# Low parts of split weights: an accumulating DMA onto a negated high part, in place of a subtraction on GpSimd

## The chip, the cores and the metric

The kernel runs on one core of a Trainium2 chip. The metric is the device time of one execution in microseconds, as a median of runs. The core has five engines that run side by side, each through its own queue in order: TensorE (PE, matrix products into PSUM, an accumulator memory), VectorE (DVE), ScalarE (ACT), GpSimd (POOL) and SyncE (SP, which here only issues DMAs). SBUF is the working memory on the core. The DMAs of all queues run on the same 16 DMA engines.

## The reference

One inference step of a transformer-like layer on 128 context tokens and 1024 latent tokens with 1024 channels. Cut to what matters here:

```
h    = rmsnorm(x, w_norm1) * (1 + scale1) + shift1
proj = h @ w_in                       # q, k, v, u (conv branch), g (gates)
o    = differential attention(q, k, v), 4 heads, then rmsnorm
cv   = silu(layernorm(dwconv31(glu(u))))
merged = sigmoid(g_a) * (o @ w_attn_proj) + sigmoid(g_b) * (cv @ w_conv_proj)
x    = x + gate1 * (merged @ w_out)
h    = rmsnorm(x, w_norm2) * (1 + scale2) + shift2
up   = dwconv3(h @ w_up)
x    = x + gate2 * ((silu(up_a) * up_b) @ w_down)
y    = rmsnorm(x, w_final)
```

All inputs and outputs are float32.

## The kernel before

Every product with weights is done in three passes of a fast format, fp32r: each operand is split into a high part (`hi`, the value rounded to fp32r) and a low part (`lo`, the rest), and `mm3` adds hi x hi, lo x hi and hi x lo in PSUM. The 1152 tokens stand in three chunks of 384 columns, n = 0, 1, 2.

Weights come as units of 128 x 1024 floats (512 KB), in the fixed order `SEQ` of 126 units: q0, k0 (first projections), ua0, ub0, ua1, ub1 (conv branch), v0 to v3, then 22 units that fill PE between the steps of attention, 4 more gate units, m0 to m7 (merge), wo0 to wo7 for the chunks 0 and 1, wo0 to wo7 a second time for chunk 2, and 66 units of the FFN (fa, fb: the two halves of w_up; d: w_down). A unit is normally 8 blocks x 3 chunks x 3 passes = 72 matmuls of 384 columns. In the first pass over wo it is 48, in the second pass 24. Counted from 0, v3 is unit 9, the second pass is units 52 to 59, and fa0, fb0, fa1, fb1 are units 60 to 63.

How a unit gets ready: `fetch_to` has SP load it into one of two `raw` buffers. `prep_to` (L153 to L155) has ACT copy raw into one of three `whi` buffers, which rounds it, and has POOL subtract, `lo = raw - hi`, into one of three `wlo` buffers (DVE does this for the first two units). The last unit's two parts stand in another buffer and are named `wlast`. A raw buffer is free for the next load when the lo part is done. A whi or wlo buffer is free when PE is done with the unit that is three earlier. `take` hands a unit to PE, and after the first chunk's matmuls (in the first pass over wo after chunk 0, in the second pass after the only chunk) `prep_to` is called for the unit two further on.

What else stands around it: in the attention stage DVE and POOL share a depthwise convolution of 31 taps (L611 on DVE, L618 on ACT with L624 on POOL). From the merge on, `ada2` (L1159) computes the remaining modulation vectors on DVE from 32 loads named `araw` that ACT's queue issues (L1148), with a custom multiply-and-sum of two operands. `resid` (L1186) adds a PSUM result to x on DVE, `square` sums squares on ACT (L1196) and DVE (L1197). `h2` makes the normalised FFN input, chunk by chunk. In the FFN `up_evac` (L1284) copies PSUM into `up` on ACT, and `glue` runs the width-3 convolution on DVE.

The order in which each engine's instructions stand is set when the program is built: a scheduler takes the code's order, its own model of how long each operation takes, and the priorities of `hp` in attention; `pin` then holds some engines close to the code's order.

Of the kernel before, what the change touches and what calls it, by code (L numbers as in the profile page):

```python
# [8 lines left out]
F32 = mybir.dt.float32  # L9
F32R = mybir.dt.float32r  # L10
AF = mybir.ActivationFunctionType
ALU = mybir.AluOpType
# [100 lines left out]
class Kernel:  # L113
# [28 lines left out]
    def prep_to(self, p):  # L142
        nc = self.nc
        while self.prepped < min(p, len(SEQ)):
            self.fetch_to(self.prepped + 1)
            raw = self.raw.pop(0)
            if self.prepped < len(SEQ) - 1:
                hi = self.wp.tile([128, 1024], F32R, tag="whi", name="whi", bufs=3)
                lo = self.wp.tile([128, 1024], F32R, tag="wlo", name="wlo", bufs=3)
            else:  # L150
                both = self.hb.tile([128, 3, 1024], F32R, tag="hb", name="wlast")
                hi, lo = both[:, 0], both[:, 1]
            nc.scalar.copy(hi, raw)  # L153
            eng = nc.vector if self.prepped < 2 else nc.gpsimd
            eng.tensor_tensor(out=lo, in0=raw, in1=hi.bitcast(F32), op=ALU.subtract)  # L155
            self.w[self.prepped] = (SEQ[self.prepped], hi, lo)
            self.prepped += 1
        self.fetch_to(self.prepped + self.fetch_ahead)
# [1402 lines left out]
```

## Time and profile before

| | us |
|---|---|
| three timed runs | 1835.44, 1835.63, 1837.52 (median 1835.63) |
| the profiled execution's own time | 1837.85 |
| its span, first to last instruction | 1836.0 |
| PE busy in it | 1726.6 (94%) |
| DVE busy | 1211.2 (66%) |
| POOL busy | 714.3 (39%) |
| ACT busy | 606.4 (33%) |

Busy time of an engine is the union of its instructions' time. Matmuls are pipelined: each row is longer than the distance to the next one, so busy PE says that something was under way. Waits and the issue of DMAs are not counted as busy. PE's granted clock has two levels, 1.2 and 2.4 GHz; a figure of 1.00 is the higher one throughout, 0.5 the lower.

### The profile page before, as it was taken

What the parts mean: (1) busy time and instruction counts of PE and PEld (TensorE: products, weight loads), DVE (VectorE), ACT (ScalarE), POOL (GpSimd) and SP (SyncE); (2) the same over time, 40 slices, a digit from 0 to 9 for tenths busy, and PEclk for the clock granted to TensorE, in tenths of its full rate; (3) what the DMA queues carried; (4) which work ended last, traced back from release to release, by engine and by line L of the source; (5) the groups of instructions that cost most, each with busy time, mean ns of one, the idle gap of its engine ahead of it and who ended that gap; (6) DMA issues with size and microseconds to landing.
All of it is one profiled execution on the core that took longest, in us unless ns stands there. A gap on an engine that the chain in (4) does not pass through costs nothing. (4 is left out here: it accounts for less than half of the span.)

```text
span 1836.0 us, 25204 instructions
## 1 busy us (share of the span) xinstructions
PE 1726.6 (94%) x10138; PEld 1685.5 (92%) x10138; DVE 1211.2 (66%) x1515; ACT 606.4 (33%) x1097; POOL 714.3 (39%) x466
## 2 busy tenths in 40 slices
PE   5989889989989999899978999999999999999997
PEld 3889889979889999799977999999999999999997
DVE  5858985697795762765989855464454635545366
ACT  4424454354553563212233312222122221221222
POOL 2545772674772422543243322222222322223231
PEclk8999999999999999999989999999999999999999
DMA  8264233433325325555641211111111111111102
GB/s 314 76 185 154 83 92 104 139 87 104 118 79 195 115 94 202 195 188 195 236 146 59 79 46 46 35 46 46 35 47 46 36 46 42 40 46 40 41 24 104
DMA packets 86172, 184.05 MB, mean 100 GB/s; under 512 B 8196, under 2 KB 56232, under 8 KB 84008
## 3 DMA queue, kind: packets, MB, share of 16 engines
q1 hardware_dynamic: 33888, 101.27, 17.0%
q10 hardware_dynamic: 51592, 79.08, 13.5%
q8 instruction: 80, 1.31, 0.3%
q0 software_dynamic: 576, 2.10, 0.3%
q14 instruction: 36, 0.29, 0.1%
HBM read 142.80 MB, written 39.60 MB: 99 GB/s over the span
## 5 line engine op out<-in xcount | busy, mean ns | idle before, releaser
L155 POOL TENSOR_TENSOR wlo<-raw,whi 128x1024 fp32r<-128x1024 f32 x123 | 309.9, 2521 | 631.8 <-ACT whi L153 524.0
L203 PE MATMUL f<-h1h,whi 128*128 128x384 f32 x680 | 232.6, 344 | 4.1 <-ACT gt L574 3.4
L203 PE MATMUL f<-h1l,whi 128*128 128x384 f32 x680 | 233.6, 344 | 0.0
L203 PE MATMUL f<-h1h,wlo 128*128 128x384 f32 x680 | 231.4, 341 | 0.0
L153 ACT CAST whi<-raw 128x1024 fp32r<-128x1024 f32 x125 | 131.3, 1051 | 299.5 <-PE f L203 123.6
L611 DVE SCALAR_TENSOR_TENSOR conv<-glu,vec,conv 128x967 f32<-128x967 f32 x120 | 199.4, 1661 | 1.1
L1289 DVE TENSOR_SCALAR ya<-up,vec 128x1153 f32<-128x1153 f32 x22 | 54.3, 2466 | 180.8 <-ACT up L1284 177.0
L203 PE MATMUL f<-h2h,whi 128*128 128x384 f32 x416 | 141.4, 340 | 6.0 <-ACT up L1284 3.7
L203 PE MATMUL T<-h2h,whi 128*128 128x384 f32 x432 | 144.4, 335 | 0.0
L203 PE MATMUL T<-h2l,whi 128*128 128x384 f32 x432 | 144.3, 334 | 0.0
L203 PE MATMUL T<-h2h,wlo 128*128 128x384 f32 x432 | 144.1, 334 | 0.0
L624 POOL TENSOR_TENSOR conv<-conv,tap 128x200 f32<-128x200 f32 x120 | 115.3, 961 | 68.6 <-ACT tap L618 66.1
L203 PE MATMUL f<-h2l,whi 128*128 128x384 f32 x416 | 140.9, 339 | 0.1
L203 PE MATMUL f<-h2h,wlo 128*128 128x384 f32 x416 | 140.5, 338 | 0.0
L203 PEld LDWEIGHTS f<-h1h,whi 128*128 128x128 f32 x680 | 129.7, 191 | 5.7 <-ACT gt L574 4.0
L203 PEld LDWEIGHTS f<-h1l,whi 128*128 128x128 f32 x680 | 130.0, 191 | 0.4
L203 PEld LDWEIGHTS f<-h1h,wlo 128*128 128x128 f32 x680 | 129.6, 191 | 0.2
L1305 POOL TENSOR_TENSOR fl<-ya,fh 128x128 fp32r<-128x128 f32 (+1 forms) x44 | 63.0, 1431 | 156.7 <-ACT fh L1304 156.7
L753 DVE TENSOR_REDUCE mx<-S 128x1 f32<-128x1152 f32 (+1 forms) x72 | 88.6, 1231 | 31.1 <-PE S L747 31.1
L1186 DVE SCALAR_TENSOR_TENSOR x<-f,g,x 128x384 f32<-128x384 f32 (+2 forms) x154 | 75.0, 507 | 48.6 <-PE f L203 45.3
L755 ACT ACTIVATE e<-S,mx 128x1152 f32<-128x1152 f32 (+1 forms) x72 | 81.3, 1129 | 70.1 <-DVE mx L753 52.7
L1289 DVE TENSOR_SCALAR yb<-up,vec 128x1153 f32<-128x1153 f32 x22 | 56.2, 2554 | 69.3 <-ACT up L1284 69.3
(332 smaller groups left out, 4651.0 us busy)
## 6 DMA issues: line engine op xcount, KB each, us to landing
raw<-in_wst SPq DMA_DIRECT2D x126, 512.0 KB, 3.6
araw<-in_ada ACTq DMA_DIRECT2D x32, 512.0 KB, 3.7
scr_gscr<-gate ACTq DMA_DIRECT2D x48, 192.0 KB, 2.0
tg<-scr_gscr SPq DMA_DIRECT2D x24, 384.0 KB, 3.9
ada<-in_ada SPq DMA_DIRECT2D x8, 1024.0 KB, 9.9
K<-scr_kscr ACTq DMA_DIRECT2D x4, 1920.0 KB, 8.8
V<-scr_vscr ACTq DMA_DIRECT2D x4, 1280.0 KB, 7.2
scr_vscr<-e ACTq DMA_DIRECT2D x36, 128.0 KB, 1.9
```

The lines of the kernel that those rows point to most:

```text
L153: nc.scalar.copy(hi, raw)
L155: eng.tensor_tensor(out=lo, in0=raw, in1=hi.bitcast(F32), op=ALU.subtract)
L203: nc.tensor.matmul(out, lhsT=a, rhs=b, start=(i == 0), stop=(i == n - 1))
L611: t = nc.vector.scalar_tensor_tensor(out=o, in0=glu[:, j:j + CSPLIT], scalar=w[:, j:j + 1], in1=o, op0=ALU.mult, op1=ALU.add)
L624: t = nc.gpsimd.tensor_tensor(out=o, in0=o, in1=p, op=ALU.add)
L753: nc.vector.tensor_reduce(out=mx[:, 1:2], in_=src, axis=AX.XY, op=ALU.min)
L755: nc.scalar.activation(out=e[:, :w].rearrange("p (a b) -> p a b", a=nk), in_=src, func=AF.Exp, scale=-1.0, bias=mx[:, 1:2], accum_out=self ...
L1186: nc.vector.scalar_tensor_tensor(out=d, in0=ps[:, o:o + ln], scalar=gate[:, j, c:c + 1], in1=d, op0=ALU.mult, op1=ALU.add)
L1289: nc.vector.tensor_scalar(out=y[:, :L], in0=u[:, 0:L], scalar1=w[:, 0:1], scalar2=None, op0=ALU.mult)
L1305: nc.gpsimd.tensor_tensor(out=fl[:, d:d + ln], in0=ya[:, s:s + ln], in1=fh[:, d:d + ln].bitcast(F32), op=ALU.subtract)
```

## The change

From the third unit on, the lo part is no longer computed by POOL. ACT writes minus the hi part into the lo buffer, and POOL's queue issues a DMA from raw to lo that adds to what stands there: lo = -hi + raw.

```
-            eng = nc.vector if self.prepped < 2 else nc.gpsimd
-            eng.tensor_tensor(out=lo, in0=raw, in1=hi.bitcast(F32), op=ALU.subtract)
+            if self.prepped < 2:
+                nc.vector.tensor_tensor(out=lo, in0=raw, in1=hi.bitcast(F32), op=ALU.subtract)
+            else:
+
+                nc.scalar.activation(out=lo, in_=hi.bitcast(F32), func=AF.Copy, scale=-1.0)
+                nc.gpsimd.dma_start(out=lo.bitcast(F32), in_=raw, accum_op=ALU.add)
```

Lines behind L155 have numbers that are higher by 4 in the changed kernel (L155 becomes L158 for the negation and L159 for the DMA).

The scheduler moves instructions with it. Below are three places.

ACT in the first units of the second pass over wo. The first CAST is the hi copy of unit 52, the others those of 53 and, in the first list, 54; `sq` are the squares of L1196, `araw` the loads of L1148. Before:

```order
L153 CAST whi_8408<-raw_8264 128x1024
L1148 DMA araw_8325<-in_ada2 128x1024
L1196 ACTIVATE sq_8366<-x1_1_7911 128x384
L1148 DMA araw_8327<-in_ada2 128x1024
L1196 ACTIVATE sq_8405<-x1_0_7910 128x384
L1148 DMA araw_8399<-in_ada2 128x1024
L153 CAST whi_8478<-raw_8338 128x1024
L1196 ACTIVATE sq_8440<-x1_1_7911 128x384
L1148 DMA araw_8401<-in_ada2 128x1024
L1196 ACTIVATE sq_8475<-x1_0_7910 128x384
L1148 DMA araw_8908<-in_ada2 128x1024
L153 CAST whi_8558<-raw_8412 128x1024
```

In the changed kernel, from the hi copy of unit 52 (whi_8458) to that of 54 (whi_8610); L158 is the negation:

```order
L153 CAST whi_8458<-raw_8313 128x1024
L1152 DMA araw_8374<-in_ada2 128x1024
L158 ACTIVATE wlo_8459<-whi_8458 128x1024
L1200 ACTIVATE sq_8416<-x1_1_7955 128x384
L1152 DMA araw_8376<-in_ada2 128x1024
L1200 ACTIVATE sq_8455<-x1_0_7954 128x384
L153 CAST whi_8529<-raw_8388 128x1024
L1152 DMA araw_8449<-in_ada2 128x1024
L158 ACTIVATE wlo_8530<-whi_8529 128x1024
L1200 ACTIVATE sq_8491<-x1_1_7955 128x384
L1152 DMA araw_8451<-in_ada2 128x1024
L153 CAST whi_8610<-raw_8463 128x1024
```

For units 52 and 53 the issue of an araw load stands between the hi copy and the negation.

ACT at the begin of the FFN. The first CAST is the hi copy of unit 63, fb1; `up` are copies out of PSUM. Before:

```order
L1148 DMA araw_9129<-in_ada2 128x1024
L153 CAST whi_9191<-raw_8904 128x1024
L1284 COPY up0_8912<-f_9084 128x384
L153 CAST whi_9195<-raw_9144 128x1024
L1284 COPY up1_8913<-T_9112 128x384
```

In the changed kernel:

```order
L1152 DMA araw_9189<-in_ada2 128x1024
L153 CAST whi_9252<-raw_8964 128x1024
L1288 COPY up0_8972<-f_9144 128x384
L153 CAST whi_9257<-raw_9205 128x1024
L1288 COPY up1_8973<-T_9172 128x384
L158 ACTIVATE wlo_9253<-whi_9252 128x1024
L158 ACTIVATE wlo_9258<-whi_9257 128x1024
```

The negation of fb1 stands behind two copies out of PSUM and the hi copy of the next unit.

POOL near unit 9, v3. The CAST of v3 is on ACT; here stand the tap additions of the convolution and the subtraction (before) or the issue of the DMA. Before:

```order
L624 TENSOR_TENSOR conv_926<-conv_926,tap_1301 128x200
L624 TENSOR_TENSOR conv_926<-conv_926,tap_1319 128x200
L155 TENSOR_TENSOR wlo_1398<-raw_966,whi_1397 128x1024
L624 TENSOR_TENSOR conv_926<-conv_926,tap_1335 128x200
L155 TENSOR_TENSOR wlo_1556<-raw_1167,whi_1555 128x1024
```

In the changed kernel:

```order
L628 TENSOR_TENSOR conv_931<-conv_931,tap_1342 128x200
L628 TENSOR_TENSOR conv_931<-conv_931,tap_1358 128x200
L159 DMA wlo_1405<-raw_972 128x1024
L628 TENSOR_TENSOR conv_931<-conv_931,tap_1377 128x200
L628 TENSOR_TENSOR conv_931<-conv_931,tap_1398 128x200
L159 DMA wlo_1564<-raw_1174 128x1024
```

The issue for v3 stands one tap addition later than the subtraction did.

## Rows read from the trace of the kernel before

**Rows 1.** The page's head and its first part: busy us of each engine, share of the span, and number of instructions.

```profile
span 1836.0 us, 25204 instructions
PE 1726.6 (94%) x10138; PEld 1685.5 (92%) x10138; DVE 1211.2 (66%) x1515; ACT 606.4 (33%) x1097; POOL 714.3 (39%) x466
```

**Rows 2.** Busy time by stage: begin and end in us, length, then busy us (and instructions) of PE, PE's weight loads, DVE, ACT and POOL, PE's granted clock, the DMA engines' busy share, GB/s. The stages are the first projections, attention, merge, the passes over wo with the begin of the FFN, and the rest of the FFN.

```profile
0.00:190.00 190.00, 158.88 (x1004) 145.33 (x1005) 137.18 (x178) 74.86 (x139) 85.48 (x83) 0.95 0.53 179
190.00:735.00 545.00, 510.62 (x3130) 495.20 (x3129) 398.12 (x456) 264.18 (x514) 291.05 (x199) 0.99 0.38 118
735.00:880.00 145.00, 131.95 (x734) 127.87 (x733) 98.15 (x133) 33.10 (x48) 65.38 (x45) 0.99 0.61 203
880.00:1040.00 160.00, 139.78 (x744) 135.64 (x743) 145.72 (x206) 53.48 (x89) 60.33 (x30) 0.91 0.41 126
1040.00:1836.00 796.00, 785.41 (x4534) 781.50 (x4532) 432.03 (x545) 180.79 (x308) 212.03 (x111) 0.99 0.14 45
```

**Rows 3.** The page's costliest groups, those of the two lines that make hi and lo: line, engine, operation, tiles, shape, count; busy us and mean ns of one; idle time of the engine just before them and what ended most of it.

```profile
L155 POOL TENSOR_TENSOR wlo<-raw,whi 128x1024 fp32r<-128x1024 f32 x123 | 309.9, 2521 | 631.8 <-ACT whi L153 524.0
L153 ACT CAST whi<-raw 128x1024 fp32r<-128x1024 f32 x125 | 131.3, 1051 | 299.5 <-PE f L203 123.6
```

**Rows 4.** PE's waits over the whole span: us in total, times, longest.

```profile
PE S L225 <- DVE mod L1159: 6.0, 1, 6.0
...
PE f L203 <- POOL wlo L155: 1.4, 1, 1.4
```

**Rows 5.** DMAs of 512 KB each. Two rows of line L1137, POOL's own plain DMAs (issue on POOL, min/median/max ns), and the time from issue to landing of the four; then, from the page's list of DMA issues, the raw loads on SP's queue with the median us to landing.

```profile
L1137 POOL DMA_DIRECT2D cbc<-in_crow x2: 551/666/782, 747.8 to 748.6; - x2
L1137 POOL DMA_DIRECT2D cbd<-in_crow x2: 540/560/580, 860.5 to 861.1; - x2
...
DMA to landing us min/median/max: 6.0/7.9/9.2
...
raw<-in_wst SPq DMA_DIRECT2D x126, 512.0 KB, 3.6
```

**Rows 6.** The table of rows 2 in windows of 10 us, five of those between 880 and 1040 us.

```profile
920.00:930.00 10.00, 7.80 (x43) 7.23 (x42) 9.96 (x17) 2.78 (x4) 2.87 (x2) 0.97 0.62 174
930.00:940.00 10.00, 5.67 (x19) 4.84 (x18) 9.96 (x12) 2.93 (x4) 6.74 (x3) 0.67 0.68 199
940.00:950.00 10.00, 6.93 (x24) 6.93 (x25) 7.64 (x11) 1.47 (x2) 5.12 (x3) 0.51 0.48 154
...
970.00:980.00 10.00, 7.99 (x47) 7.48 (x46) 8.90 (x10) 2.42 (x4) 6.50 (x4) 1.00 0.31 105
...
990.00:1000.00 10.00, 5.69 (x27) 5.18 (x28) 8.22 (x16) 3.37 (x6) 2.80 (x2) 0.88 0.18 54
```

**Rows 7.** DVE's groups between 880 and 1040 us, the costliest: columns as in rows 3.

```profile
L1159 DVE CUSTOM_DVE_ANT_0 S<-araw,cbd,vec 128x1024 f32<-128x1024 f32 x41 | 70.6, 1721 | 4.1 <-DMA araw<-in_ada 3.8
```

**Rows 8.** The timeline (start us, duration us, engine, line, operation, tiles) for an FFN unit in mid-program, d4_0: POOL's subtraction and PE's second and third matmul of the unit, the third being the first with the lo part.

```profile
1342.28 2.38 POOL L155 TENSOR_TENSOR wlo<-raw,whi 128x1024 fp32r<-128x1024 f32 x1 [10.10 <-ACT whi L153]
...
1366.21 0.33 PE L203 MATMUL T<-fl,whi 128*128 128x384 f32 x1
1366.38 0.33 PE L203 MATMUL T<-fh,wlo 128*128 128x384 f32 x1
```

**Rows 9.** The timeline near ub0: the hi copy of the unit behind it (ua1), and the matmul of ub0 that first uses its lo part.

```profile
81.66 1.07 ACT L153 CAST whi<-raw 128x1024 fp32r<-128x1024 f32 x1
...
89.96 0.33 PE L203 MATMUL f<-h1h,wlo 128*128 128x384 f32 x1
```

**Rows 10.** The timeline near v3: its hi copy, the tap behind it on ACT, and the matmul that first uses its lo part.

```profile
160.23 1.04 ACT L153 CAST whi<-raw 128x1024 fp32r<-128x1024 f32 x1
161.17 0.46 ACT L618 ACTIVATE tap<-glu,vec 128x200 f32<-128x200 f32 x1
...
168.71 0.28 PE L967 MATMUL f<-wlo,h1h 128*128 128x256 f32 x1
```

**Rows 11.** The timeline in the second pass over wo: subtractions of units 52 and 53 on POOL, two operations of one line on DVE, SP's issues of the raw loads of 54 and 55, ACT's hi copy of 53, and PE's first matmul of fa0.

```profile
909.58 3.50 POOL L155 TENSOR_TENSOR wlo<-raw,whi 128x1024 fp32r<-128x1024 f32 x1 [6.79 <-ACT whi L153]
...
911.26 2.90 DVE L1159 CUSTOM_DVE_ANT_0 S<-araw,cbd,vec 128x1024 f32<-128x1024 f32 x1
913.10 0.33 SPq L138 DMA_DIRECT2D raw<-in_wst  x1
914.56 1.28 DVE L1159 CUSTOM_DVE_ANT_0 S<-araw,cbd,vec 128x1024 f32<-128x1024 f32 x1
...
919.62 1.06 ACT L153 CAST whi<-raw 128x1024 fp32r<-128x1024 f32 x1 [1.12 <-DVE acc L1197]
920.76 2.40 POOL L155 TENSOR_TENSOR wlo<-raw,whi 128x1024 fp32r<-128x1024 f32 x1 [7.69 <-ACT whi L153]
923.19 0.33 SPq L138 DMA_DIRECT2D raw<-in_wst  x1
...
970.02 0.33 PE L203 MATMUL T<-h2h,whi 128*128 128x384 f32 x1
```

**Rows 12.** The timeline at fb1: the hi copy of the unit behind it, the copy out of PSUM behind that, and the first matmul of fb1 that uses its lo part.

```profile
1016.39 1.05 ACT L153 CAST whi<-raw 128x1024 fp32r<-128x1024 f32 x1
1017.34 0.48 ACT L1284 COPY up<-T 128x384 f32<-128x384 f32 x1
...
1020.89 0.33 PE L203 MATMUL f<-h2h,wlo 128*128 128x384 f32 x1
```

## The prediction

> **What bounds the kernel now.** The page comes first. The span is 1836.0 us, TensorE (PE) is busy 94% of it, GpSimd (POOL) 39% and ScalarE (ACT) 33% [rows 1]. The second view is the table by stage: PE is busy 785 of the last 796 us, but loses 31, 34, 13 and 20 us in the four stages ahead of it (stage length less PE busy) [rows 2]. What the change is worth must be read from those four. The groups then price what goes: 123 subtractions of 2521 ns on POOL under L155 (a 124th has another name), each behind a 1051 ns copy on ACT under L153 [rows 3]. PE's waits say how much of these 310 us anybody waits for: 1.4 us, once; a wait for VectorE (DVE) of 6.0 us is larger [rows 4]. So POOL's subtraction is off the path, and its time there is worth nothing to PE directly. Two things are left that can move the time: when a lo part is ready, and what POOL does to DVE meanwhile.
>
> **What the change removes.** A steady unit of the FFN first: its subtraction ends at 1342.28 + 2.38 = 1344.7 us, and PE's first matmul with that lo part starts at 1366.38, so it lies ready for 21.7 us. Its row and the one ahead stand 0.17 us apart: a unit of 72 matmuls lasts 12.5 us, one of 24 matmuls 4.2 us [rows 8]. Half the program therefore neither gains nor loses by some 15 us of lo latency.
>
> The gain is on DVE. From 880 to 1040 us it is busy 9.9 of 10 us in many windows, and PE idles 2.2, 4.3 and 3.1 us in the three windows from 920, 2.0 from 970 and 4.3 from 990 [rows 6]. One of its custom operations with an SBUF operand pair takes 1.28 us at 914.56, but 2.90 us at 911.26, where it lies under a subtraction of POOL that ends at 913.08 [rows 11]. The 41 of this kind in the stretch sum to 70.6 us [rows 7]; at 1.28 us each they would be 52.5. So 18 us of DVE time come free in the stretch where DVE is the bound. PE can get back at most what it idles in the five windows, 15.9 us.
>
> **What the change adds.** ACT gets 124 more operations over 128x1024. The nearest row is the copy of the same size, 1.05 us [rows 3], so 130 us on an engine that idles two thirds of the span. In the attention stage ACT is busy 264 of 545 us [rows 2] and gets some 26 of them, 27 us: at worst each delays a softmax by 1.05 us, at best DVE's relief there pays for it. I take zero for that stage.
>
> POOL issues 124 DMAs instead; its issue row is 0.54 to 0.78 us [rows 5]. What such a transfer takes until it has landed is the number on which all hangs. No accumulating DMA is in the trace. From below: the raw load of the same 512 KB on SP's queue lands 3.6 us after its issue. The nearest row: POOL's own four plain DMAs of 512 KB landed after 6.0 to 9.2 us, median 7.9 [rows 5]. From above: twice that, 15.8, if the transfer must pass twice. I take 7.9, because its queue and size are the same.
>
> The Trainium skill has a price (DMA: Bandwidth & Descriptors, section Anatomy of one DMA): about 2.0 us and the bytes at 436 GB/s for a DMA issued from GpSimd. By it, as an estimate, 512 KB would be 3.2 us, and the sum would be that of the first rival below. The trace's 6.0 to 9.2 us disagrees with it.
>
> So a lo part is ready 1.05 (hi) + 1.05 (negation) + 0.2 (two hand-overs) + 7.9 = 10.2 us after its hi copy starts, against 3.6 us now. Four places have less slack than that.
>
> *ub0.* In the new order the negation stands behind the next unit's hi copy, which ends at 81.66 + 1.07 = 82.73 [rows 9]. Negation to 83.8, landing at 91.8. PE takes this lo part at 89.96: **+1.8 us**.
>
> *v3.* The hi copy ends at 161.27, a tap of 0.46 us goes ahead of the negation, which ends at 162.7; landing at 170.7, with POOL's tap additions ahead taken as hidden. PE needs it at 168.71 [rows 10]: **+2.0 us**.
>
> *Second pass over wo.* Eight units of 4.2 us each, and there are only two raw buffers. SP's issue at 913.10 is the moment at which the subtraction of 909.58 + 3.50 ends, and 923.19 that of 920.76 + 2.40 [rows 11]: a raw buffer is handed on when the lo part is done. This stays so, but the hold gets longer: 3.6 (load) + 10.2 = 13.8 us for each second unit, 6.9 us a unit against PE's 4.2. From the hi copy at 919.62, unit 53 is ready at 929.8, 55 at 943.6, 57 at 957.4 and 59 at 971.2; PE finishes that at 975.4, and could start fa0 then instead of at 970.02 [rows 11]: **+5.4 us**. In the new order ACT also issues an ada2 load between hi copy and negation of 52 and 53, which can wait for DVE; DVE's relief should bring these issues forward by about as much, so I add nothing. While the buffers are the bound here, the 18 us of DVE time buy nothing in the first three windows.
>
> *fb1.* Its hi buffer comes free when fa0 is done, with 24 matmuls of fa1 to cover the rest. The new ACT order is hi, up copy, hi of fa2, up copy, negation. The second up copy ends at 1017.34 + 0.48 = 1017.8, so negation to 1018.9 and landing at 1026.9; PE wants it at 1020.89 [rows 12]: **+6.0 us**. An earlier end of fa0 moves both sides and does not shorten this wait.
>
> *Relief behind the second pass.* Of the 6.3 us idle in the windows from 970 and 990 I give back **-5 us**: DVE is behind by less when PE arrives later.
>
> **Sum.** 1.8 + 2.0 + 5.4 + 6.0 - 5 = +10.2 us. The rows are of an execution of 1837.85 us (span 1836.0), 2.2 above the median 1835.63 of the three timed runs. 1837.85 + 10.2 = 1848.0, less 2.2 is about **1845 us** as a median. 0.2%, which is 3.7 us, is about what a measurement of this kernel can tell from no change.
>
> **The landing decides.** One us of it counts once at ub0, v3 and fb1, and four times in the second pass (the hi copy of 53 and three rounds), 7 us together. At 6.4 us the sum is zero. At 3.6 us, ub0 and v3 cost nothing, fb1 1.7, the buffers no longer bind in the second pass, and up to 15.9 us of PE's idle time come back: -14 us, 1822. At 15.8 us the terms are 9.7, 9.9, 13.9 and 37, less 5: +65 us, 1901.
>
> **Rivals.**
> First, *DVE's relief wins*: landing of 5.5 us or less. The place is 880 to 1040 us, the gain 18 us of DVE, of which up to 15.9 reach PE; it decides from a landing of 6.4 us downward, and at 5.5 or less gives 1822 to 1832. For it: both source and target lie in SBUF, and loads on the other queue land in 3.6 us. Against it: all four DMAs of POOL's queue took 6.0 us or more.
> Second, *they cancel*: landing near 6.4 us, the lowest POOL row (6.0) with a little for the addition. Time 1836. For it speaks that the row of 7.9 includes DMAs that queued behind one another.
> Third, *the transfer passes twice*: landing of 10 us or more, the second pass at 8 us a unit and more, 1858 to 1900. FFN still has cover: 21.7 us of slack against at most 18.1 - 3.6 = 14.5 more. For it: an addition needs the old content of lo as well as raw. Against it: that nothing in the rows shows how much of 7.9 us is data.
> The Trainium skill states it as a rule (Collectives: The Full Stack, section The bandwidth ceiling): an add in the DMA needs two source reads on one ring, and ran at half the rate of a copy. By it the third rival holds in so far as the data are the larger part of 7.9 us; no row separates them.
>
> **How the numbers follow.** Forecast, slower with a landing of 7 to 10 us: 0.40, with 1839 to 1858 as its own range. Third rival 0.15. Cancel 0.17. Relief wins 0.28, since the 6.4 us at which the sum turns lie only 1.5 us under the price taken, less than the 3.2 us by which the four DMAs differ [rows 5]. That makes faster 0.28, same 0.17, slower 0.55. The range goes from 1823, which leaves out the lowest part of the first rival, to 1868, which is a landing of about 11 us and leaves out most of the third.
>
> **What the next profile would show.** If I am right: the issues of wlo on POOL's queue land in 7 to 10 us; among PE's waits that transfer stands at the start of fb1 with some 6 us and in the second pass; the custom operation under L1159 falls from a mean of 1.72 to about 1.3 us, and FFN's first DVE operation under L1289 gets shorter without any gain there; PE's busy time after 1040 us stays at 99% of its stage. Wrong would be: a landing under 6.4 us with no wait at fb1; a landing that grows when other queues are busy (around 870 us), which would open a fifth place in the first pass over wo; or softmax rows in the attention stage that start later because of the negations, which I priced at zero.

## The result and the profile after

The changed kernel takes 1853.12 us (median of four executions, 1850.04 to 1858.27) against 1836.04 for the kernel before (1835.44 to 1837.52). The ratio is 1.0094, 95% interval 1.0076 to 1.0112: **slower by 17 us**, inside the forecast range, and 8 us above the forecast of 1845. The profiled execution took 1853.93 us.

First the page's head, two of its DMA queues (packets, MB, share of 16 engines' span; q0 is POOL's queue, q1 holds the raw loads among others) and its rows for what is new, as in [rows 1, 3, 5]:

```profile
span 1852.2 us, 25501 instructions
...
PE 1726.4 (93%) x10138; PEld 1688.0 (91%) x10138; DVE 1071.2 (58%) x1515; ACT 728.3 (39%) x1221; POOL 491.5 (27%) x466
...
q0 software_dynamic: 18432, 67.12, 18.9%
q1 hardware_dynamic: 33888, 101.27, 16.8%
...
L159 POOL DMA_DIRECT2D wlo<-raw x123 | 107.9, 877 | 838.5 <-ACT wlo L158 779.0
...
L158 ACT ACTIVATE wlo<-whi 128x1024 fp32r<-128x1024 f32 x123 | 130.4, 1061 | 6.8 <-issue 4.3
...
wlo<-raw POOLq DMA_DIRECT2D x123, 512.0 KB, 4.8
```

The three prices to note: a negation 1.06 us, an issue 0.88 us, and a landing of 4.8 us in the median. DVE is busy 140 us less than before, POOL 223 us less. And yet the kernel is slower, with a landing well under the 6.4 us at which the prediction's sum turned. So the reader should distrust that sum at once, and look for where the time went.

Next the stages, as in [rows 2], the last three:

```profile
735.00:880.00 145.00, 131.12 (x728) 128.63 (x727) 78.48 (x126) 45.00 (x58) 47.55 (x44) 0.98 0.80 235
880.00:1040.00 160.00, 136.54 (x725) 132.01 (x724) 109.85 (x201) 67.98 (x100) 25.73 (x27) 0.94 0.70 195
1040.00:1852.00 812.00, 800.18 (x4620) 799.32 (x4618) 373.13 (x559) 251.31 (x383) 126.52 (x116) 0.99 0.37 88
```

The DMA engines' busy share is 0.80, 0.70 and 0.37 where it was 0.61, 0.41 and 0.14 [rows 2]. Per MB the accumulating queue costs 18.9 / 67.12 against 16.8 / 101.27 of the raw loads' queue, 1.70 times as much engine time. From 1100 to 1800 us, where q1 holds little but raw loads, it is 22.5 / 29.89 against 13.6 / 28.84, 1.60 times.

Then PE's waits, as in [rows 4]:

```profile
PE T L783 <- DVE atl L787: 11.6, 7, 5.4
PE O L798 <- DVE atl L787: 8.6, 2, 7.6
PE f L207 <- DMA wlo<-raw: 8.1, 3, 3.3
PE T L207 <- DMA wlo<-raw: 6.5, 4, 2.4
...
PE O L207 <- DMA wlo<-raw: 2.1, 2, 1.1
```

The transfers are waited for 16.7 us in all; two long waits of 5.4 and 7.6 us are for DVE, in the attention stage.

Fixed windows mislead when stages shift, so the time is set out by the first matmul of each stage. For the merge, the first pass over wo and the FFN begin these are, in the timeline after:

```profile
744.68 0.33 PE L207 MATMUL O<-coh,whi 128*128 128x384 f32 x1
...
863.62 0.33 PE L207 MATMUL f<-mh,whi 128*128 128x384 f32 x1
...
995.00 0.33 PE L207 MATMUL T<-h2h,whi 128*128 128x384 f32 x1
```

Worked out in the same way for every kernel of this study (us; each from one profiled execution; "DVE" is the longest operation of DVE from 190 to 725 us, "issues" the DMAs that POOL issues from 196 to 725 us):

| kernel | up to merge | merge | wo first | wo second | fa0 to first fh | rest of FFN | last matmul ends | DVE | issues |
|---|---|---|---|---|---|---|---|---|---|
| before | 734.1 | 118.0 | 66.6 | 51.4 | 94.4 | 763.9 | 1828.3 | 3.51 | 0 |
| changed | 744.7 | 118.9 | 76.5 | 54.9 | 90.1 | 759.3 | 1844.4 | 12.12 | 23 |
| e1 POOL in 44 to 63 | 747.0 | 128.1 | 66.6 | 51.5 | 87.6 | 758.9 | 1839.7 | 12.50 | 23 |
| e2 POOL in 10 to 35 | 730.3 | 120.2 | 75.6 | 54.2 | 85.0 | 759.6 | 1824.9 | 3.51 | 1 |
| e3 POOL adds | 737.8 | 117.5 | 66.6 | 45.8 | 96.8 | 768.9 | 1833.3 | 3.49 | 0 |
| e4 from HBM | 748.0 | 126.8 | 74.1 | 36.4 | 95.9 | 759.6 | 1840.8 | 6.84 | 23 |
| e5 tiny DMAs, POOL | 754.7 | 120.3 | 66.6 | 51.5 | 94.3 | 764.3 | 1851.6 | 7.80 | 25 |
| e6 light araw | 745.2 | 119.2 | 71.8 | 38.1 | 92.2 | 759.7 | 1826.2 | 12.51 | 23 |
| e7 mixture, from 52 | 730.6 | 117.1 | 66.6 | 42.6 | 92.3 | 759.6 | 1808.8 | 3.50 | 0 |
| e8 mixture, from 48 | 731.0 | 117.8 | 70.5 | 39.8 | 94.9 | 759.7 | 1813.6 | 3.50 | 0 |
| e9 mixture, raw | 729.7 | 116.3 | 66.6 | 59.0 | 86.0 | 759.4 | 1817.0 | 3.51 | 0 |
| e10 tiny DMAs, SP | 741.0 | 115.1 | 66.6 | 51.8 | 92.9 | 765.4 | 1832.8 | 3.50 | 0 |
| e11 POOL adds in 10 to 35 | 735.4 | 123.9 | 75.7 | 55.0 | 84.6 | 759.6 | 1834.2 | 3.49 | 1 |

The profiled execution is not always near the median of its kernel: those of e4 and e2 are the shortest of theirs (7.3 and 4.2 us under the median), those of e8 and e1 lie 5.3 and 3.0 us over it. A difference of a few us in one column is that of single executions.

By this table the changed kernel loses 10.6 us ahead of the merge, 0.9 in it, 9.9 in the first pass over wo and 3.5 in the second, and wins 4.3 and 4.6 us behind: 16 us in the profiled executions.

**Ahead of the merge** the two long waits for DVE lead to one place each. The timeline at the longer one, POOL and DVE:

```profile
519.80 0.87 POOL L159 DMA_DIRECT2D wlo<-raw  x1 [0.57 <-ACT wlo L158]
...
520.41 2.20 POOL L522 TENSOR_TENSOR sw<-sw,cst 128x1024 f32<-128x1024 f32 x1
520.55 12.12 DVE L615 SCALAR_TENSOR_TENSOR conv<-glu,vec,conv 128x967 f32<-128x967 f32 x1
522.28 2.20 POOL L522 TENSOR_TENSOR xs<-xs,cst 128x1024 f32<-128x1024 f32 x1
524.15 0.81 POOL L628 TENSOR_TENSOR conv<-conv,tap 128x200 f32<-128x200 f32 x1
524.64 2.27 POOL L522 TENSOR_TENSOR sw<-sw,cst 128x1024 f32<-128x1024 f32 x1
526.59 2.27 POOL L522 TENSOR_TENSOR xs<-xs,cst 128x1024 f32<-128x1024 f32 x1
528.55 0.80 POOL L628 TENSOR_TENSOR conv<-conv,tap 128x200 f32<-128x200 f32 x1
529.04 2.59 POOL L526 TENSOR_TENSOR xs<-xs,sw 128x1024 f32<-128x1024 f32 x1
...
533.39 1.21 DVE L615 SCALAR_TENSOR_TENSOR conv<-glu,vec,conv 128x967 f32<-128x967 f32 x1
```

A convolution tap on DVE, 1.21 us when alone, takes 12.12: it starts 0.14 us behind a POOL operation and ends 1.04 us after the last of a chain of seven on POOL (529.04 + 2.59 = 531.63). The chain starts where POOL issues a DMA. In the kernel before the same two engines took turns: the longest such tap was 3.45 us. The other place is at 341.91 us: the first tap (L612, with one large SBUF operand, 0.72 us at its shortest) takes 6.85 us under four operations of a POOL chain that follows an issue at 334.77. Under the same chain, at 338.28, DVE's softmax operation (L770) still got its turn and took 2.44 us, so an issue does not always bring a shut-out. The Trainium skill (SBUF — State Buffer, section Summary: rules for kernel authors) says that of DVE with two SBUF inputs and GpSimd the second to issue is blocked until the first has finished. The trace agrees on the blocking, but here it lasts for seven operations, not for one.

**In the first pass over wo** the DMA engines are full for most of the time. Windows of 10 us, columns as in [rows 2]:

```profile
880.00:890.00 10.00, 9.43 (x55) 9.11 (x53) 4.19 (x6) 5.36 (x7) 0.88 (x1) 1.00 1.03 408
890.00:900.00 10.00, 5.89 (x19) 5.28 (x20) 5.56 (x10) 2.94 (x5) 0.87 (x1) 0.73 1.05 310
900.00:910.00 10.00, 10.00 (x56) 10.00 (x55) 7.79 (x14) 3.76 (x5) 0.57 (x1) 0.93 0.53 195
```

Share 1.03 and 1.05 around 890 us, 19 matmuls in a window that holds 60, at a granted clock of 0.73. Over the whole first pass the share is 0.86, against 0.72 before. Between 870 and 970 us the transfers of lo land late:

```profile
L159 POOL DMA_DIRECT2D wlo<-raw x11: 851/860/920, 886.8 to 970.0; - x11
...
DMA to landing us min/median/max: 5.0/6.9/8.7
```

against the same two rows of the FFN (1100 to 1800 us):

```profile
L159 POOL DMA_DIRECT2D wlo<-raw x56: 860/862/887, 1100.0 to 1787.0; - x56
...
DMA to landing us min/median/max: 4.5/4.5/5.9
```

### The profile page after: what moved, and what is told of

The parts are those of the page before. It is cut to its first block, busy times and chain, and to the rows that moved or that the text cites. A ratio compares the mean times of both kernels' runs of the same rounds, so it can differ in the third digit from the quotient of the medians.

```text
span 1852.2 us, 25501 instructions
## 1 busy us (share of the span) xinstructions
PE 1726.4 (93%) x10138; PEld 1688.0 (91%) x10138; DVE 1071.2 (58%) x1515; ACT 728.3 (39%) x1221; POOL 491.5 (27%) x466
## 3 DMA queue, kind: packets, MB, share of 16 engines
q0 software_dynamic: 18432, 67.12, 18.9%
q1 hardware_dynamic: 33888, 101.27, 16.8%
q10 hardware_dynamic: 51592, 79.08, 13.3%
## 4 chain that ended last, share of the span: by engine, by line
PE 59%; DMA 12%; DVE 9%; issue 6%; POOL 6%; ACT 5%; ACTq 2%; POOLq 0%; DVEq 0%; SPq 0%
PE f L207 26%; PE T L207 18%; PE O L207 9%; DMA wlo<-raw 4%; DVE conv L615 3%; DMA raw<-in_wst 2%; DMA tg<-scr_gscr 2%; POOL conv L628 2%; PE O L798 2%; DMA scr_gscr<-gate 1%; DVE mx L757 1%; PE S L750 1%; ACT tap L622 1%; PE S L751 1%; DVE mn L265 1%
## 5 line engine op out<-in xcount | busy, mean ns | idle before, releaser
L159 POOL DMA_DIRECT2D wlo<-raw x123 | 107.9, 877 | 838.5 <-ACT wlo L158 779.0
L615 DVE SCALAR_TENSOR_TENSOR conv<-glu,vec,conv 128x967 f32<-128x967 f32 x120 | 188.2, 1568 | 1.2
L628 POOL TENSOR_TENSOR conv<-conv,tap 128x200 f32<-128x200 f32 x120 | 106.7, 889 | 106.4 <-ACT tap L622 106.0
L1293 DVE TENSOR_SCALAR ya<-up,vec 128x1153 f32<-128x1153 f32 x22 | 18.1, 822 | 200.7 <-ACT up L1288 194.9
L158 ACT ACTIVATE wlo<-whi 128x1024 fp32r<-128x1024 f32 x123 | 130.4, 1061 | 6.8 <-issue 4.3
L1190 DVE SCALAR_TENSOR_TENSOR x<-T,g,x 128x384 f32<-128x384 f32 (+2 forms) x146 | 72.0, 512 | 49.4 <-PE T L207 48.7
```

What stands on the lines that cost most here:

```text
L158: nc.scalar.activation(out=lo, in_=hi.bitcast(F32), func=AF.Copy, scale=-1.0)
L159: nc.gpsimd.dma_start(out=lo.bitcast(F32), in_=raw, accum_op=ALU.add)
L615: t = nc.vector.scalar_tensor_tensor(out=o, in0=glu[:, j:j + CSPLIT], scalar=w[:, j:j + 1], in1=o, op0=ALU.mult, op1=ALU.add)
L628: t = nc.gpsimd.tensor_tensor(out=o, in0=o, in1=p, op=ALU.add)
L1190: nc.vector.scalar_tensor_tensor(out=d, in0=ps[:, o:o + ln], scalar=gate[:, j, c:c + 1], in1=d, op0=ALU.mult, op1=ALU.add)
```

## The experiments

Three causes were set against one another. A: POOL's DMA issues shut DVE out in the attention stage. B: ACT's added negations delay that stage. C: transfers and raw buffers in the passes over wo. Each diff is against the changed kernel unless it says otherwise.

**e1.** Units 44 to 63 back to POOL.

```
+            elif 44 <= self.prepped < 64:
+                nc.gpsimd.tensor_tensor(out=lo, in0=raw, in1=hi.bitcast(F32), op=ALU.subtract)
             else:
```

> As the changed kernel, but units 44 to 63 (both passes over wo, fa0 to fb1) keep POOL's subtraction; all others use negation and accumulating DMA. Theory C (in the passes over wo the 16 DMA engines are full, so raw loads and lo parts land late): the stretch from PE's first matmul with mh to its first with h2h goes from 131.4 us back to about 118, raw loads there land in 3.6 us again, DMA share between 900 and 960 falls from 0.9 to about 0.6; the delay of 10.6 us at the first coh matmul stays; time about 1843. Theory A (the loss sits in attention alone and the passes only carry it on): the passes stay long, time about 1853.

Measured 1846.3 us, ratio 1.0055 (1.0036 to 1.0074). C holds for the passes: 66.6 and 51.5, those of before. Of the 13.3 us won there, 9 went again in the merge, whose length is 128.1 instead of 118.9. PE's waits there:

```profile
PE O L208 <- DVE tg L1115: 9.6, 2, 5.5
```

PE waits 5.5 us at once for a gate operation that starts at 799.2 us, 12.0 us after the issue of the load it waits for, beside an accumulating DMA that took 10.9 us to land (issued at 787 and 788 us). This is read from the profiled execution, 1849.26 us; two of the four executions took 1843.1 and 1843.4, what theory C gave. The merge was 126.8 us in e4 as well, and 115 to 120 in ten of the other eleven kernels: such a collision comes and goes with the order, and no run settles what decides it.

**e2.** Units 10 to 35 (attention) back to POOL.

```
+            elif 10 <= self.prepped < 36:
+                nc.gpsimd.tensor_tensor(out=lo, in0=raw, in1=hi.bitcast(F32), op=ALU.subtract)
```

> As the changed kernel, but units 10 to 35 (the attention stage) keep POOL's subtraction. Theory A (a POOL chain directly behind a DMA issue shuts DVE out: 6.85 us at 342 and 12.12 us at 520) and theory B (26 negations of 1.06 us on ACT delay the softmax) both expect the first coh matmul back at 734 us, give or take 4, instead of 744.7, no DVE operation over 4 us before 700 us, time about 1842.5. Theory C alone (only the passes over wo matter): 744 stays or the gain is lost again, time about 1853.

Measured 1838.67 us, 1.0016 (1.0007 to 1.0026). The merge begins at 730.3, 14.4 us earlier; no DVE operation above 3.51. The attention stage was more than half of the loss. A and B both foresaw it.

**e3.** The negation stays, POOL adds instead of the DMA (everywhere).

```
-                nc.gpsimd.dma_start(out=lo.bitcast(F32), in_=raw, accum_op=ALU.add)
+                nc.gpsimd.tensor_tensor(out=lo, in0=raw, in1=lo.bitcast(F32), op=ALU.add)
```

> ACT writes minus hi into lo as in the changed kernel, but POOL adds raw with an ordinary two-input operation instead of the accumulating DMA. It has ACT's whole added work and none of the DMA. Theory B (ACT's negations are the cost in attention): first coh matmul near 744, time 1846 or more. Theories A and C (DMA issue ahead of POOL chains; DMA engines full): first coh matmul within 4 us of 734, passes over wo as before (118 us), about 2 us lost at fb1, time 1836 to 1840.

Measured 1844.16 us, 1.0045 (1.0028 to 1.0062), above what A and C gave. The merge begins at 737.8 (3.7 late), the passes are as short as before or shorter, no long DVE operation. So B has a share, but the smaller one. Unforeseen: the FFN takes 5 us more than before. POOL's two-input work is still there and starts later; what exactly is late was not followed.

**e11.** The same in units 10 to 35 only.

```
+            elif 10 <= self.prepped < 36:
+                nc.scalar.activation(out=lo, in_=hi.bitcast(F32), func=AF.Copy, scale=-1.0)
+                nc.gpsimd.tensor_tensor(out=lo, in0=raw, in1=lo.bitcast(F32), op=ALU.add)
```

> As the changed kernel, but in units 10 to 35 POOL adds raw onto ACT's negated hi part with an ordinary operation; the DMA is gone there, ACT's 26 negations stay. It splits the 14.4 us that lie at the first coh matmul between the changed kernel (744.7) and the one with POOL's subtraction in the attention stage (730.3). Theory A (the issues on POOL): first coh matmul at 730 to 736, most of the 14.4 us gone, time 1838 to 1843. Theory B (ACT's negations): 741 or later, time 1848 or more.

Measured 1844.84 us, 1.0048 (1.0031 to 1.0065). The merge begins at 735.4. Of the 14.4 us, 9.3 go with the DMA and 5.1 stay with the negations. A is the larger part, as expected; the time is 2 us above A's bound, since the merge took 123.9.

**e5.** Against the kernel before: its subtraction stays, and POOL issues a tiny DMA behind it in units 10 to 35.

```
             eng.tensor_tensor(out=lo, in0=raw, in1=hi.bitcast(F32), op=ALU.subtract)
+            if 10 <= self.prepped < 36:
+                tiny = self.sm.tile([128, 1], F32, tag="tiny", name="tiny", bufs=2)
+                nc.gpsimd.dma_start(out=tiny, in_=lo[:, 0:1].bitcast(F32))
```

> The kernel before with its subtraction, and behind each subtraction of units 10 to 35 a DMA on POOL's queue that copies one column of lo (128 x 1 floats) into an unused tile: it adds to the attention stage an issue on POOL and nothing else, no ACT work, no transfer worth counting, no later lo part. Theory A (POOL operations that follow a DMA issue without a gap shut DVE out until their chain ends): at least one DVE operation of more than 4 us between 190 and 735 us, beside a POOL chain whose operations start 0.2 to 0.35 us ahead of the end of the one in front; first coh matmul 4 to 10 us later than 734, time 1839 to 1846. Without theory A (the two long DVE operations came of ACT, of the landing, or of the new order): none over 4 us there, first coh matmul at 734 give or take 3, time 1835 to 1838.

Measured 1861.11 us, 1.0135 (1.0117 to 1.0153): 25 issues of some 0.58 us, with the new order of instructions that they bring, cost 25 us, far more than A gave. Three DVE operations of 5.1, 5.4 and 7.8 us; the last, with POOL beside it:

```profile
356.30 0.69 POOL L158 DMA_DIRECT2D tiny<-wlo  x1
...
357.97 2.01 POOL L521 TENSOR_TENSOR sw<-sw,cst 128x1024 f32<-128x1024 f32 x1
357.99 7.80 DVE L614 SCALAR_TENSOR_TENSOR conv<-glu,vec,conv 128x967 f32<-128x967 f32 x1
359.94 1.99 POOL L521 TENSOR_TENSOR xs<-xs,cst 128x1024 f32<-128x1024 f32 x1
361.90 0.53 POOL L627 TENSOR_TENSOR conv<-conv,tap 128x200 f32<-128x200 f32 x1
362.40 2.36 POOL L525 TENSOR_TENSOR xs<-xs,sw 128x1024 f32<-128x1024 f32 x1
```

The expected overlap of 0.2 to 0.35 us within the POOL chain, which the changed kernel shows, is not there (357.97 + 2.01 = 359.98, next at 359.94). So that overlap is not the mechanism; the shut-out goes without it.

**e10.** The same tiny copies on SP's queue; against e5:

```
-                nc.gpsimd.dma_start(out=tiny, in_=lo[:, 0:1].bitcast(F32))
+                nc.sync.dma_start(out=tiny, in_=lo[:, 0:1].bitcast(F32))
```

> The same one-column copies from lo behind the subtractions of units 10 to 35 as in the run with tiny DMAs (1861 us), but issued by SP's queue in place of POOL's. Transfer, order in the code and what they wait for are the same; only POOL's issue is gone. If the issue on POOL is what shuts DVE out: no DVE operation over 4 us between 190 and 735, first coh matmul at 734 give or take 4, time 1834 to 1842. If the transfer or the changed schedule did it: shut-outs stay, first coh matmul after 745, time 1850 or more.

Measured 1842.69 us, 1.0045 (1.0030 to 1.0060), 18 us less than e5. The row of the convolution taps from 190 to 735 us (min, median, max ns), of the kernel before, of e5 and of e10:

```profile
L611 DVE SCALAR_TENSOR_TENSOR conv<-glu,vec,conv x87: 1209/1386/3447, 190.2 to 566.3; 128x967 f32<-128x967 f32 x87
```

```profile
L614 DVE SCALAR_TENSOR_TENSOR conv<-glu,vec,conv x87: 1207/1385/7798, 189.6 to 587.5; 128x967 f32<-128x967 f32 x87
```

```profile
L614 DVE SCALAR_TENSOR_TENSOR conv<-glu,vec,conv x87: 1198/1390/3444, 189.7 to 564.0; 128x967 f32<-128x967 f32 x87
```

The long operations are gone with POOL's issue. The merge still begins 7 us late; the matmul with K and q at seven eighths of the stage starts at 638.1 us (638.6 before), so these 7 us arise behind it: from 690 to 745 us PE waits 5.6 us for gate operations of ACT (L580), where the kernel before has no such wait. Why these are late was not followed. Over all thirteen kernels the table's last two columns agree: 23 or 25 issues, a DVE operation of 6.8 to 12.5 us; none or one, at most 3.51.

One rival is left. In the traces POOL's operations from 190 to 725 us stand in another order in e5 than before (38 of 194 stand ahead of others that they followed), while in e10 all but one stand as before. So e10 takes away the issue and the new order together, and no run has the one without the other. The traces speak against the order. Take, from 190 to 725 us in all thirteen kernels, the chains of at least four POOL operations one right behind another, 5 us or longer (24 with an issue in them, 61 without): beside the 61 no DVE operation takes over 3.51 us; beside 11 of the 24 one takes 4.2 us or more. (The changed kernel, e1 and e6 share one order on POOL, so that these 11 are not all independent.) That the issue makes the shut-out is thus well supported, but not isolated; what makes it in some chains and not in others is open.

**e4.** The DMA adds the unit from HBM, so that raw is free after the hi copy.

```
-                nc.gpsimd.dma_start(out=lo.bitcast(F32), in_=raw, accum_op=ALU.add)
+                nc.gpsimd.dma_start(out=lo, in_=self.A["wst"][ROW[SEQ[self.prepped]]].bitcast(F32R), accum_op=ALU.add)
```

> As the changed kernel, but the accumulating DMA reads the weight unit from HBM a second time instead of from the raw buffer, so that raw is free as soon as the hi copy is done. If the loss in the passes over wo comes from the raw buffer that is held until the lo part has landed, the stretch from first mh to first h2h matmul shrinks from 131.4 to 118 to 122 us and the time is about 1842. If the 16 DMA engines are full there (theory C in its strict form), the stretch stays at 128 us or more and the time at 1850 to 1856. The attention stage should show the same kind of POOL chain behind a DMA issue: its DVE stalls over 4 us may come or go with the order.

Measured 1857.84 us, 1.0110 (1.0089 to 1.0131); the profiled execution, with a span of 1848.5, was its shortest. Both forms of C are half right: the second pass falls from 54.9 to 36.4, so the held raw buffer bounds it; the first pass stays at 74.1. Both together are 110.5 us, less than the 118 to 122 that the buffers alone were to bring. The merge ate the gain (126.8), and lo lands later:

```profile
L159 POOL DMA_DIRECT2D wlo<-in_wst x12: 857/864/923, 880.0 to 969.7; - x12
...
DMA to landing us min/median/max: 5.7/8.6/12.1
```

**e6.** The 24 later araw loads (`light0` is 8) bring a quarter of their bytes; the lines by which DVE reads that quarter four times are left out here.

```
-                self.nc.scalar.dma_start(out=raw, in_=self.A["ada2"][self.ada_fetched])
+                if self.ada_fetched >= self.light0:
+                    self.nc.scalar.dma_start(out=raw[:, :256], in_=self.A["ada2"][self.ada_fetched][:, :256])
+                else:
+                    self.nc.scalar.dma_start(out=raw, in_=self.A["ada2"][self.ada_fetched])
...
```

> As the changed kernel, but the 24 araw loads issued from the passes over wo on bring 128 KB each instead of 512 KB (DVE reads the same quarter four times, so three quarters of these modulation sums are left out). DVE's instructions, the raw buffers and the lo transfers stay. Theory C in its strict form (the 16 DMA engines are full in the first pass over wo): first pass 66.6 to 70 us instead of 76.5, lo parts there land in 4.5 to 6 us instead of 5.6 to 8.7, time 1842 to 1847. If the first pass is long because a raw buffer is held until lo has landed, at whatever traffic: 74 us or more, time 1850 or more.

Measured 1838.41 us, 1.0015 (0.9999 to 1.0030), less than either theory gave. First pass 71.8 (between the two), lo landings there

```profile
L160 POOL DMA_DIRECT2D wlo<-raw x12: 851/861/917, 886.8 to 964.9; - x12
...
DMA to landing us min/median/max: 4.5/5.2/7.4
```

and the second pass 38.1 instead of 54.9. Less traffic shortens both passes, with unchanged buffers: full DMA engines and the held buffer act through one another, since the hold is the landing. The first pass is not down to 66.6; the x loads, issued from 869 to 885 us, are still there, which may be the reason, but was not tested.

**e7.** A mixture: POOL in units 10 to 51, the DMA from HBM in 52 to 63, from raw in 2 to 9 and from 64 on.

```
+            elif 10 <= self.prepped < 52:
+                nc.gpsimd.tensor_tensor(out=lo, in0=raw, in1=hi.bitcast(F32), op=ALU.subtract)
...
+                if 52 <= self.prepped < 64:
+                    nc.gpsimd.dma_start(out=lo, in_=self.A["wst"][ROW[SEQ[self.prepped]]].bitcast(F32R),
+                                        accum_op=ALU.add)
```

> A mixture from the runs so far: units 2 to 9 and 64 on negation and accumulating DMA from raw, units 10 to 51 (attention, merge, first pass over wo) POOL's subtraction, units 52 to 63 (second pass, begin of the FFN) negation and accumulating DMA from HBM, which lets raw go after the hi copy. Expected from the stretches measured: first coh matmul at 730, merge 118, first pass 66.6, second pass 36 to 48 (51.4 before; DVE may still be behind from the first pass), fa0 to first fh 85 to 95, FFN 759.5: time 1812 to 1828, faster than before. If DVE's backlog of the first pass alone sets the second pass, it stays at 51 and the time is 1830 to 1835.

Measured **1818.51 us**, 0.9903 (0.9887 to 0.9919): faster than both kernels, each stage within what was expected.

**e8.** The same with HBM from unit 48; against e7:

```
-            elif 10 <= self.prepped < 52:
+            elif 10 <= self.prepped < 48:
...
-                if 52 <= self.prepped < 64:
+                if 48 <= self.prepped < 64:
```

> As the mixture of the run beside it, but with the accumulating DMA from HBM from unit 48 on (the second half of the first pass over wo). If full DMA engines are what stretches the first pass only near its begin (x loads and four araw loads at once, 870 to 900 us), the first pass stays at 67 to 69 us, DVE enters the second pass with less behind it and the time is 2 to 6 us under that of the run beside it. If the engines are full through the whole first pass, it is 70 to 74 us and the time is the same or higher.

Measured 1817.83 us, 0.9896 (0.9872 to 0.9919), the same as e7. The first pass is 70.5, with a DMA share of 0.94 over its whole length, so the engines are full in its second half too; the second pass gives most of it back (39.8).

**e9.** As e7, but units 52 to 63 add from raw; against e7:

```
-                if 52 <= self.prepped < 64:
-                    nc.gpsimd.dma_start(out=lo, in_=self.A["wst"][ROW[SEQ[self.prepped]]].bitcast(F32R),
-                                        accum_op=ALU.add)
```

> As the mixture with the accumulating DMA from HBM in units 52 to 63 (1818.5 us, second pass over wo 42.6 us), but those units too add from the raw buffer, which is then held until the lo part has landed. The prediction's step on the raw buffers (hi, negation, landing and the next load in one ring of two) expects a second pass of 50 us or more, against 51.4 before, and a time 7 to 12 us above that mixture. If the hold costs little once the first pass leaves the DMA engines free, the second pass stays at 42 to 45 us and the time within 3 us of it.

Measured 1826.98 us, 0.9957 (0.9943 to 0.9971), 8.5 above e7. The second pass is 59.0 against 42.6. SP's waits from 905 to 1000 us, first of e9, then of e7:

```profile
SPq L138 <- DMA wlo<-raw: 115.3, 12, 31.8
```

```profile
SPq L138 <- ACT whi L153: 50.9, 11, 9.1
```

In e9 the next raw load waits for the transfer of lo, in e7 for the hi copy. (The window reaches into the FFN; within the second pass alone it is 68.8 us in nine waits against 37.6 us in eight.) That is the ring of two buffers that the prediction described.

## Why the prediction was right or wrong

**The landing** was the number on which all hung, taken as 7.9 us. Mis-sized: 4.5 us in the FFN, 6.9 in the passes over wo, 4.8 over all (medians). One number for all places was the error; the landing follows the load of the DMA engines. The rule that a landing under 6.4 us makes the kernel faster falls with it: at 4.8 us it is 17 us slower.

**ub0 and v3** (+1.8, +2.0): nothing. The stretch runs 2 us ahead of before, and no wait of PE for a transfer over 0.8 us lies there.

**Second pass over wo** (+5.4): right in mechanism, +3.5 us against before; e9 and e7 show the hold of the raw buffers to be worth 16.4 us. The "18 us of DVE time" that "buy nothing" while the buffers bind fit this too: with the buffers free the pass falls to 42.6 or 36.4 us, under the 51.4 of before.

**fb1** (+6.0): right to the instruction, half in size. The chain at fb1:

```profile
1039.28 2.02 ACT L158 ACTIVATE wlo<-whi 128x1024 fp32r<-128x1024 f32 x2
...
1040.64 1.82 POOL L159 DMA_DIRECT2D wlo<-raw  x2 [29.00 <-ACT wlo L158]
...
1045.38 0.29 PEld L207 LDWEIGHTS f<-h2h,wlo 128*128 128x128 f32 x1 [3.04 <-DMA wlo<-raw]
1045.39 0.69 PE L207 MATMUL f<-h2h,wlo 128*128 128x384 f32 x1 [2.72 <-DMA wlo<-raw]
```

The negation stands behind two copies and a hi copy, as foreseen, and PE waits 2.7 us. With a landing of 4.8 in place of 7.9 the prediction's own sum gives 6.0 - 3.1 = 2.9.

**DVE's relief** (-5): the custom operation fell as foreseen, from the mean of 1721 ns [rows 7] to

```profile
L1163 DVE CUSTOM_DVE_ANT_0 S<-araw,cbd,vec 128x1024 f32<-128x1024 f32 x37 | 47.7, 1289 | 0.4
```

and the stretch from fa0 to the first fh is 4.3 us shorter in spite of fb1's wait, so that the relief is worth some 7 us there.

**FFN** ("neither gains nor loses"): wrong, -4.6 us. L1293 takes 822 ns where L1289 took 2466, but that is not what counts. In the kernel before PE stands still for a moment at each pair of d units; DVE and PE there:

```profile
1301.90 0.47 DVE L1186 SCALAR_TENSOR_TENSOR x<-T,g,x 128x256 f32<-128x256 f32 x1
...
1302.08 0.34 PE L203 MATMUL f<-fh,wlo 128*128 128x384 f32 x1
...
1302.52 0.41 PE L203 MATMUL T<-fh,whi 128*128 128x384 f32 x1
```

PE starts 0.44 us after the matmul ahead instead of 0.17, and the next follows after 0.25: some 0.35 us at each of ten places. The changed kernel has none above 0.26 in the FFN but four at its very end, which the kernel before has too. All kernels with the DMA in the FFN take 758.9 to 759.7 us, all with POOL's work there 763.9 or more. That DVE frees a PSUM buffer too late (its operation ends at 1302.37) is read from these rows, not tested.

**Attention** (zero): the first of the two large misses, 12.7 us from the first matmul with K and q to the merge. Of the prediction's "at worst each delays a softmax by 1.05" the negations' part came true, 5.1 us by e11. The other part it did not see: a DMA issue on POOL was priced at its own 0.54 to 0.78 us, but what it does to the operations behind it on POOL, and so to DVE, costs more (the rows at 520 us; e5 and e10, with the rival of the order left).

**First pass over wo** (zero): the second, 9.9 us. The prediction named it only as something that would prove it wrong, "a landing that grows when other queues are busy (around 870 us)". It had the DMA share in its rows (0.62 and 0.68 at 920 and 930 us, [rows 6]) but added no traffic to it.

So two of the reasons for slower were there (fb1 and the raw buffers, worth 6 us together), but DVE's relief took back as much: what the prediction had priced at 10.2 us measured 3.5 - 4.3 = -0.8, with ub0 and v3 at nothing. What it had at zero measured 10.6 + 0.9 + 9.9 - 4.6 = 16.8. That the time lies in the range is therefore luck in good part; the loss comes from two causes outside the sum.

The rule of the Trainium skill that an add needs two source reads and ran at half the rate of a copy (Collectives: The Full Stack, section The bandwidth ceiling) is near the 1.70 times the engine time per MB measured here; it told of the traffic, and the prediction used it for the landing alone.

## What to carry to other kernels

Work that is moved from an engine to a DMA is also traffic: add its engine time to the DMA share of each stage, and expect its landing to grow where that nears one. Ask what buffer the transfer's source holds meanwhile; reading from where the source came from can be the better choice although it moves the bytes twice. And apply such a change where its rows favour it, stage by stage: here the same DMA loses in attention and in the first pass, and wins in the FFN and, from HBM, in the second pass, so that the mixture is 1% faster than before while the whole change is 1% slower.

## What was unexpected of the hardware

Some DMA issues on POOL's queue of under 0.9 us, even of a 128 x 1 copy, were followed by chains of POOL operations that kept a DVE operation waiting, so that it took up to 12.51 us (e6), where the two engines otherwise took turns of at most 3.51. With the same copies issued from SP there was nothing of the kind, though POOL's order changed with the queue. An accumulating DMA of 512 KB within SBUF landed in 4.5 us with the DMA engines at a share of 0.36, sooner than the 6.0 to 9.2 us of POOL's four plain DMAs before [rows 5], which read from HBM, two of them at 860 us, where the share was 0.98.
